# A macaron decoder layer: the feed-forward products by 2x2 blocks with seven block products, and the first input normed ahead of its products

## The chip, the core and the metric

One core of one Trainium2 chip runs the kernel. The metric is the device time of an execution in microseconds (us). Engines: PE (TensorE, matmuls; PEld its weight loads), DVE (VectorE), ACT (ScalarE), POOL (GpSimd), and SP, which issues most DMAs.

## The reference

One layer over 512 tokens of width 1024, all float32:

```python
def swiglu(x, w_gate, w_up, w_down):
    return (jax.nn.silu(x @ w_gate) * (x @ w_up)) @ w_down
...
        h = rmsnorm(x, ffn1_pre_g[l])
        x = x + FFN_RES * rmsnorm(swiglu(h, ffn1_w_gate[l], ffn1_w_up[l], ffn1_w_down[l]), ffn1_post_g[l])
        h = rmsnorm(x, mix_pre_g[l])
        p = h @ w_in[l]
...
        y = jnp.concatenate([y_rwkv, y_diff], axis=-1) @ w_o[l]
        x = x + rmsnorm(y, mix_post_g[l])
        h = rmsnorm(x, ffn2_pre_g[l])
        x = x + FFN_RES * rmsnorm(swiglu(h, ffn2_w_gate[l], ffn2_w_up[l], ffn2_w_down[l]), ffn2_post_g[l])
```

The feed-forward parts (FFN1 and FFN2) have a hidden width of 2816. Between them stands a mixer: one projection, RWKV-7 heads, differential attention heads, and one output projection.

## The kernel before

Every matmul operand is split into a high and a low part (float32r), `hi + lo`, by ACT (the copy `hi`) and DVE (the difference `lo`) in `split` and `split_to` (L192/L193 for weights, L198/L199 for activations). A product is then three matmuls, hi·hi, hi·lo, lo·hi (`mm3`, L204 to L206). The weights come from DRAM through two buffers `raw` of 128x1024 on SP's queue (`load_w`, L175), are split, and wait in three pairs `whi`, `wlo`.

Tokens and features are tiled by 128. In FFN1 and FFN2 the gate and the up product (`gu`) run over 22 feature tiles, two products each over 8 k tiles, with the weights as the stationary operand and 512 tokens as the moving one. `gate_up` (L319) forms silu(gate)·up from the two PSUM banks and splits it into `ah` and `al`. The down product (`block`) runs over the 22 feature tiles as k tiles, each for 4 token tiles and 2 column halves of 512, into eight PSUM banks `y`. The last k tiles are taken token tile by token tile (`tail`), so that the norms of one tile (`norms`, L246: square sums on ACT, z = y·gain and the residual sum `xo` on DVE, norm, transposes by PE into the next operand) run beside the products of the next.

FFN1 starts on x transposed in DRAM (`xt`): `ffn1_start` (L371) scales it by the gain, splits it and multiplies at once; the tokens' 1/rms is found beside it, with square sums on POOL (L403, L405), and multiplied in after the product (`rbc`). The mixer's first four projections and FFN2's first four tiles are done by token halves (`early`, L351, products of 256 columns), so that the first half needs the norms of two token tiles only. Some weights at these places are split on POOL (L190, L193).

`Streams` keeps several generators of steps, in order of priority, with planned times; it sets the order in which instructions are written. The framework takes this order as a priority and may let a later instruction go ahead whose operands it expects earlier; each engine then executes its own queue in order.

## Time and profile before

| | us |
|---|---|
| median of 3 runs | 1164.03 |
| lowest and highest | 1162.4, 1164.34 |
| span of the profiled execution | 1162.5 |
| FFN1, from the first product to the first of the projections | 5.2 to 387.8 |
| mixer and output projection | to 775.9 |
| FFN2, to its last product | to 1154.6 |

The page and the trace are of one profiled execution. Its span runs from its first to its last instruction. PE's busy time contains the overlap of pipelined matmuls, so that a pace is read from the starts or from counts in a stretch. A row of the timeline gives the start, the duration, engine, line, operation, what it writes and reads, and in brackets the engine's idle time before it.

### The profile page before, as it was taken

What the parts mean: (1) busy time and instruction counts of PE and PEld (TensorE: products, weight loads), DVE (VectorE), ACT (ScalarE), POOL (GpSimd) and SP (SyncE); (2) the same over time, 40 slices, a digit from 0 to 9 for tenths busy, and PEclk for the clock granted to TensorE, in tenths of its full rate; (3) what the DMA queues carried; (4) which work ended last, traced back from release to release, by engine and by line L of the source; (5) the groups of instructions that cost most, each with busy time, mean ns of one, the idle gap of its engine ahead of it and who ended that gap; (6) DMA issues with size and microseconds to landing.
All of it is one profiled execution on the core that took longest, in us unless ns stands there. A gap on an engine that the chain in (4) does not pass through costs nothing.

```text
span 1162.5 us, 13940 instructions
## 1 busy us (share of the span) xinstructions
PE 1119.6 (96%) x5600; PEld 889.2 (76%) x5600; DVE 553.4 (48%) x889; ACT 378.4 (33%) x630; POOL 149.3 (13%) x92
## 2 busy tenths in 40 slices
PE   7999999999999899999799999989999999999997
PEld 5888888888887876787576776669888888888885
DVE  7544444442224763787636758474333333332224
ACT  4423322232123474222332336343232222221123
POOL 5000000000004234344320200430000000000000
PEclk9999999999999999899889989998999999999999
DMA  7332222332223422223321203424222232223322
GB/s 261 109 99 96 91 91 98 100 93 91 91 99 119 150 74 73 59 48 117 90 57 46 62 22 127 140 101 138 93 91 91 95 104 91 91 91 96 104 91 91
DMA packets 49697, 112.46 MB, mean 97 GB/s; under 512 B 21336, under 2 KB 21720, under 8 KB 49632
## 3 DMA queue, kind: packets, MB, share of 16 engines
q1 hardware_dynamic: 46304, 104.15, 27.9%
q10 hardware_dynamic: 2608, 5.28, 1.3%
q0 software_dynamic: 720, 2.13, 0.6%
q8 instruction: 44, 0.72, 0.2%
q14 instruction: 21, 0.17, 0.0%
HBM read 102.14 MB, written 7.34 MB: 94 GB/s over the span
## 4 chain that ended last, share of the span: by engine, by line
PE 86%; DVE 8%; ACT 2%; DMA 2%; issue 1%; POOL 0%; SPq 0%; DVEq 0%; ACTq 0%; POOLq 0%
PE gu L205 13%; PE gu L206 13%; PE gu L204 13%; PE y L204 7%; PE y L205 7%; PE y L206 7%; PE pj L204 3%; PE pj L205 3%; PE pj L206 3%; PE sc L1151 2%; DVE tmp L935 1%; DVE xo L267 1%; PE Y L1037 1%; PE Y L1036 1%; PE s L889 1%; PE op L1179 1%
## 5 line engine op out<-in xcount | busy, mean ns | idle before, releaser
L192 ACT ACTIVATE whi<-raw 128x1024 fp32r<-128x1024 f32 x154 | 163.2, 1060 | 530.6 <-PE gu L205 222.4
L193 DVE TENSOR_TENSOR wlo<-raw,whi 128x1024 fp32r<-128x1024 f32 x130 | 163.9, 1262 | 249.2 <-ACT whi L192 247.0
L204 PE MATMUL gu<-h,whi 128*128 128x512 f32 x672 | 266.4, 397 | 5.2 <-ACT h L393 5.2
L205 PE MATMUL gu<-h,whi 128*128 128x512 f32 x672 | 267.1, 398 | 2.6 <-DVE h L396 2.6
L206 PE MATMUL gu<-h,wlo 128*128 128x512 f32 x672 | 266.3, 396 | 0.3 <-DVE wlo L193 0.3
L204 PEld LDWEIGHTS gu<-h,whi 128*128 128x128 f32 x672 | 127.3, 189 | 34.8 <-ACT h L393 5.2
L205 PEld LDWEIGHTS gu<-h,whi 128*128 128x128 f32 x672 | 127.2, 189 | 34.8 <-DVE h L396 5.5
L206 PEld LDWEIGHTS gu<-h,wlo 128*128 128x128 f32 x672 | 127.3, 189 | 30.1 <-DVE wlo L193 0.8
L204 PE MATMUL y<-whi,ah 128*128 128x512 f32 x336 | 132.7, 395 | 0.0
L206 PE MATMUL y<-whi,al 128*128 128x512 f32 x336 | 132.6, 395 | 0.0
L205 PE MATMUL y<-wlo,ah 128*128 128x512 f32 x336 | 132.5, 394 | 0.0
L193 POOL TENSOR_TENSOR wlo<-raw,whi 128x1024 fp32r<-128x1024 f32 (+1 forms) x29 | 70.7, 2442 | 107.7 <-ACT whi L192 107.5
L204 PE MATMUL pj<-hm,whi 128*128 128x512 f32 x184 | 80.7, 439 | 0.0
L205 PE MATMUL pj<-hm,whi 128*128 128x512 f32 x184 | 77.7, 422 | 0.0
L206 PE MATMUL pj<-hm,wlo 128*128 128x512 f32 x184 | 76.5, 416 | 0.0
L205 PEld LDWEIGHTS y<-wlo,ah 128*128 128x128 f32 x336 | 63.3, 188 | 14.8
L206 PEld LDWEIGHTS y<-whi,al 128*128 128x128 f32 x336 | 63.3, 188 | 14.8
L204 PEld LDWEIGHTS y<-whi,ah 128*128 128x128 f32 x336 | 63.3, 188 | 14.5
L190 POOL TENSOR_TENSOR whi<-raw,zero 128x1024 fp32r<-128x1024 f32 (+1 forms) x5 | 9.4, 1898 | 377.4 <-PE y L206 361.7
L325 DVE TENSOR_TENSOR sa<-gu,sa 128x512 f32<-128x512 f32 x22 | 15.2, 692 | 77.0 <-PE gu L206 70.3
L204 PEld LDWEIGHTS pj<-hm,whi 128*128 128x128 f32 x184 | 37.2, 202 | 12.7 <-issue 4.9
L329 DVE TENSOR_TENSOR sa<-gu,rbc 128x512 f32<-128x512 f32 x22 | 15.2, 690 | 66.0 <-PE gu L206 66.0
(325 smaller groups left out, 1404.8 us busy)
## 6 DMA issues: line engine op xcount, KB each, us to landing
raw<-in_wgu SPq DMA_DIRECT2D x82, 512.0 KB, 3.4
raw<-in_wd SPq DMA_DIRECT2D x44, 512.0 KB, 3.4
raw<-in_win SPq DMA_DIRECT2D x27, 512.0 KB, 3.5
xd<-xo SPq DMA_DIRECT2D x8, 512.0 KB, 2.8
raw<-in_wo SPq DMA_DIRECT2D x8, 512.0 KB, 3.5
xo<-xd SPq DMA_DIRECT2D x8, 512.0 KB, 4.3
xt<-in_xt SPq DMA_DIRECT2D x8, 256.0 KB, 5.4
xo<-in_x SPq DMA_DIRECT2D x4, 512.0 KB, 5.2
```

The source lines that it names most:

```text
L192: nc.scalar.activation(hi[:, :m], src, AF.Copy)
L193: (eng or nc.vector).tensor_tensor(out=lo[:, :m], in0=src, in1=hi[:, :m], op=ALU.subtract)
L204: mm(ps, lhsT=a[0], rhs=b[0], start=first, stop=False)
L205: mm(ps, lhsT=a[0], rhs=b[1], start=False, stop=False)
L206: mm(ps, lhsT=a[1], rhs=b[0], start=False, stop=last)
L267: nc.vector.scalar_tensor_tensor(out=xo[:, hs[i]], in0=z[:, hs[i]], scalar=r, in1=xo[:, hs[i]], op0=ALU.mult, op1=ALU.add)
L325: nc.vector.tensor_tensor(out=a, in0=ps[1], in1=s, op=ALU.mult)
L329: nc.vector.tensor_tensor(out=a, in0=ps[1], in1=rbc, op=ALU.mult)
L889: nc.tensor.matmul(pv[:, i, :, :], lhsT=BK[rs, c, :, :], rhs=self.XR[p][rs, c, e:e + 2, :], start=True, stop=True)
L935: nc.vector.tensor_tensor(out=tv, in0=a, in1=b, op=ALU.mult)
L1036: mm(yo, lhsT=XR[p][rs, c, 1, :], rhs=SV[rs, p, i, :], start=True, stop=False)
L1151: mm(sc[:, 0:n], lhsT=q[rs, t * P:(t + 1) * P], rhs=k_[rs, 0:n], start=True, stop=False)
```

## The change

Each FFN product is done as 2x2 blocks by the Strassen-Winograd scheme: seven block products instead of eight, with sums and differences of blocks ahead and behind. A new class `FFN` does this.

Gate and up: the moving operand is cut in two halves of k (4 k tiles each) and two halves of the tokens (256), the weights in the same halves of k and in pairs of feature tiles m and m + 11. The seven operands (`B11`, `T1`, `T2`, `B21`, `T3`, `B22`, `T4`) are formed once, by `feat`, from the transposed norm. The weight sums are formed by POOL for each pair and product (`g_weights`, p = 5, 6, 7, 3), then split by ACT and DVE (`parts`), three slots ahead (`AHEAD`). A slot is 4 k tiles x 3 matmuls of 256 columns, and there are 14 for a pair (7 products, gate and up). Products are accumulated in PSUM where the scheme adds them (p = 1, 6, 7, 4 share a bank), the rest is added by DVE in `g_out`.

Down: the activations are kept in float32 (`F`), cut in two halves of the tokens and two of k (11 tiles each), the weights in halves of columns. POOL forms the weight differences in place (`Tw`) and the activation sums in groups of four k tiles (`d_group`), ACT and DVE split them. A unit is one k tile of one product: 2 token tiles x 3 matmuls of 512 columns; the phases are (1,5) interleaved, 6, 2, (7,3) interleaved, 4. The first two token tiles are finished at the end of (7,3), the last two at the end of 4.

FFN1 no longer reads the transposed x: each token tile is loaded, normed, transposed and split like the other inputs (`start`), its products begin when the first two tiles are there, and `rbc`, `ffn1_start`, `token_scale` and `gate_up` are gone. FFN2's early tiles and their splitting on POOL are gone as well; the first projection's weights (`e0`) are requested after FFN1's last product. The output projection takes its last three k tiles by token tiles, not the last five. FFN's weights get six raw buffers (`RAWS`).

The diff, cut to its core:

```diff
...
-    a["xt"] = np.ascontiguousarray(g["x"].T).reshape(KT, P, T)
...
-        hi = pool.tile([P, n], F32R, tag=tag + "hi", name=tag + "hi")
-        lo = pool.tile([P, n], F32R, tag=tag + "lo", name=tag + "lo")
+        if tag == "w":
+            hi, lo = (pool.tile([P, n], F32R, tag="w", name=f"w{x}", bufs=6) for x in ("hi", "lo"))
+        else:
+            hi = pool.tile([P, n], F32R, tag=tag + "hi", name=tag + "hi")
+            lo = pool.tile([P, n], F32R, tag=tag + "lo", name=tag + "lo")
...
+        if feat is not None:
+            nc.vector.tensor_scalar(out=z, in0=xo, scalar1=r, scalar2=None, op0=ALU.mult)
+            yield 0.0, 0.8
+            yield from feat(t, z, tb)
+            S.mark(f"{key}z{t}")
+            S.mark(f"{key}h{t}", 1.2)
+            return
...
-            h1 = self.feature(hp, "h1")
-            with tc.tile_pool(name="a1", bufs=1, reuse_waits="tile") as ap, \
-                    tc.tile_pool(name="t1", bufs=1, reuse_waits="tile") as tp:
-                acts = [None] * NF
-                for f in range(NF):
-                    if f == 0:
-                        ps0, acc = self.ffn1_start(h1, bp, tp)
...
+                f1 = FFN(self, 1, fp, bp, hp, hx)
+                f1.inputs()
                 for t in range(NT):
-                    S.add(self.norms(S, br, t, "f", ys[t], True, A["x"], self.xd, hm, (0, 1)))
-                S.add(self.tail(S, "f", range(NT), kts[-nt:], acts, ws, ys, False, True))
-                for t in range(3):
-                    self.fetch(br, t, A["x"])
+                    S.add(f1.start(t, A["x"]))
+                S.add(f1.stream())
...
+                for t in range(NT):
+                    S.add(tail1(t))
+                S.run("f")
+                xst.close()
                 e0 = self.load_w(A["win"][0], nc.gpsimd, alone=True)
...
+            f2 = FFN(self, 2, fp, fp, hp, hx)
+            f2.inputs()
+            br = self.bridge(f2.bridge_tile(), fp, "pgm")
...
-            nt = 5
+            nt = 3
...
+            S.add(f2.stream())
...
+    NP = NF // 2
+    AHEAD = 3
+    LAG = 4
+    HS = "xppxpxp"
...
+    def parts(self, src, dst, lo=None):
+        nc = self.nc
+        nc.scalar.activation(dst[0], src, AF.Copy)
+        (lo or nc.vector).tensor_tensor(out=dst[1], in0=src, in1=dst[0], op=ALU.subtract)
...
+        x = self.x0[:, t * D:(t + 1) * D]
+        junk = self.x0[:, 4 * D:5 * D]
+        nc.sync.dma_start(out=x, in_=src[t * P:(t + 1) * P, :])
+        if t < 2:
+            self.load(0, t, 0)
+        else:
+            for j in range(2):
+                self.load(0, j, 1) if t == 3 else None
+        yield 0.0, 2.0
+        r = L.rms(x, junk, "p")
+        yield 0.0, 2.5
+        nc.vector.tensor_scalar(out=x, in0=x, scalar1=r, scalar2=None, op0=ALU.mult)
+        yield 0.0, 0.6
+        yield from self.feat(t, x, (4, 5) if t < 2 else (0, 1))
+        S.mark(f"oh{t}", 1.2)
...
+            hv = self.h32[:, q * 2 + half, :, cs]
+            g = L.fv[:, o + q * 4:o + q * 4 + 4].unsqueeze(2).to_broadcast([P, 4, P])
+            nc.vector.tensor_tensor(out=hv, in0=pt.rearrange("p (k t) -> p k t", k=4), in1=g, op=ALU.mult)
+            if half == 0:
+                self.parts(hv, dst(("B11", "B21")[q]))
+            yield 0.42, 0.3 if q == 0 else 0.0
+        if half == 0:
+            return
+        B11, B12, B21, B22 = (self.h32[:, i, :, cs] for i in range(4))
+        t1, t2, t3, t4 = (self.gsum(p).rearrange("p (k t) -> p k t", k=4) for p in (3, 3, 7, 7))
+        tt = lambda e, o, a, b: e.tensor_tensor(out=o, in0=a, in1=b, op=ALU.subtract)
+        tt(nc.vector, t1, B12, B11)
+        self.parts(t1, dst("T1"))
+        tt(nc.gpsimd, t2, B22, t1)
+        self.parts(t2, dst("T2"))
+        self.parts(B22, dst("B22"))
+        tt(nc.gpsimd, t3, B22, B12)
+        self.parts(t3, dst("T3"))
+        tt(nc.gpsimd, t4, B21, t2)
...
+    RAWS = 6
+    ALPHA, BETA, GAMMA = ((4, 5), (2, 3)), (6, 7), (0, 1)
+    OPERAND = {1: "B11", 2: "B21", 3: "B22", 4: "T4", 5: "T1", 6: "T2", 7: "T3"}
...
+        if p == 1:
+            return raw(0)[:, lo]
+        if p == 2:
+            return raw(0)[:, hi]
+        if p == 4:
+            return raw(1)[:, hi]
+        s = self.gsum(p)
+        tt = lambda a, b, op: nc.gpsimd.tensor_tensor(out=s, in0=a, in1=b, op=op)
+        if p == 5:
+            tt(raw(1)[:, lo], raw(1)[:, hi], ALU.add)
+        elif p == 6:
+            tt(self.s[j][5], raw(0)[:, lo], ALU.subtract)
+        elif p == 7:
+            tt(raw(0)[:, lo], raw(1)[:, lo], ALU.subtract)
+        else:
+            tt(raw(0)[:, hi], self.s[j][6], ALU.subtract)
+        self.s[j][p] = s
+        return s
...
+        out = [(0, 1), (0, 2), (1, 1), (1, 2), (0, 5), (0, 6), (0, 3), (0, 7), (1, 5), (0, 4), (1, 6), (1, 3), (1, 7),
+               (2, 1), (1, 4)]
+        for m in range(2, self.NP):
+            out += [(m, p) for p in (5, 6, 2, 7, 3)]
+            out += [(m + 1, 1)] if m + 1 < self.NP else []
+            out.append((m, 4))
+        return [(m, p, j) for m, p in out for j in range(2)]
...
+        for k in range(4):
+            ks = slice(k * P, (k + 1) * P)
+            mm(ps, lhsT=w[:, 0, ks], rhs=B[:, 0, k], start=p in (1, 2, 5) and k == 0, stop=False, skip_group_check=True)
+            mm(ps, lhsT=w[:, 0, ks], rhs=B[:, 1, k], start=False, stop=False, skip_group_check=True)
+            mm(ps, lhsT=w[:, 1, ks], rhs=B[:, 0, k], start=False, stop=k == 3, skip_group_check=True)
...
+        if p == 6:
+            nc.scalar.activation(c0[:, 1], ps, AF.Copy)
+        elif p == 2:
+            add(c0[:, 0])
+        elif p == 7:
+            add(c1[:, 1])
+            if j == 0:
+                nc.scalar.activation(c1[:, 1], c1[:, 1], AF.Silu)
+        elif p == 3:
+            add(c0[:, 1])
+            if j == 0:
+                nc.scalar.activation(c0, c0, AF.Silu)
+            else:
+                nc.vector.tensor_tensor(out=self.F[0][:, :, m], in0=c0, in1=self.c[m, 0, 0], op=ALU.mult)
+        elif j == 0:
+            nc.scalar.activation(c1[:, 0], ps, AF.Silu)
+        else:
+            g1 = self.c[m, 0, 1]
+            nc.gpsimd.tensor_tensor(out=self.F[1][:, 1, m], in0=c1[:, 1], in1=g1[:, 1], op=ALU.mult)
+            nc.vector.tensor_tensor(out=self.F[1][:, 0, m], in0=ps, in1=g1[:, 0], op=ALU.mult)
...
+        for ph in ((1, 5), (6,), (2,), (7, 3), (4,)):
+            if len(ph) == 1:
+                out += [(ph[0], k) for k in range(n)]
+                continue
+            for k in range(n + g):
+                out += [(ph[0], k)] if k < n else []
+                out += [(ph[1], k - g)] if k >= g else []
...
+        if p == 1:
+            raw = self.fp.tile([P, 1024], F32, tag="raw", name="raw", bufs=self.RAWS)
+            nc.sync.dma_start(out=raw, in_=self.wd[k])
+            self.raw[k] = raw
+            return raw[:, lo]
+        if p == 5 or p == 4:
+            return self.Tw[:, k]
+        if p in (6, 2):
+            if k % 2 == 0:
+                self.raw[p, k // 2] = self.d_raw(k, *((n + i, int(p == 6)) for i in range(k, min(k + 2, n))))
+            src = self.raw[p, k // 2][:, (lo, hi)[k % 2]]
+            if p == 6:
+                sub(self.Tw[:, k], src, self.Tw[:, k])
+                return self.Tw[:, k]
+            return src
+        if p == 7:
+            self.raw["c", k] = raw = self.d_raw(k, (k, 1), (n + k, 1))
+            sub(raw[:, lo], raw[:, hi], raw[:, lo])
+            return raw[:, lo]
+        return self.raw["c", k][:, hi]
...
+        if p == 5:
+            tt(a21, a21, a22, ALU.add)
+        elif p == 6:
+            tt(a21, a21, a11)
+        elif p == 7:
+            tt(a11, a22, a21)
+        elif p == 3:
+            tt(a21, a12, a21)
+        src = {1: a11, 2: a12, 4: a22, 5: a21, 6: a21, 7: a11, 3: a21}[p]
+        t = self.hslot("a")
+        self.parts(src, (t[:, 0, 0:n], t[:, 1, 0:n]))
...
+        for t in tts:
+            ts = slice(t * P, (t + 1) * P)
+            a = [A[:, i, k % 4, ts] for i in range(2)]
+            mm(ps[t], lhsT=a[0], rhs=w[:, 0], start=p in (1, 2, 5) and k == 0, stop=False, skip_group_check=True)
+            mm(ps[t], lhsT=a[0], rhs=w[:, 1], start=False, stop=False, skip_group_check=True)
+            mm(ps[t], lhsT=a[1], rhs=w[:, 0], start=False, stop=k == n - 1, skip_group_check=True)
...
+            ahead(i + self.AHEAD)
+            self.g_product(m, p, j, ws.pop(i))
+            self.g_out(m, p, j)
+            yield 1.43, 0.0
...
+                if p == 1:
+                    nc.gpsimd.tensor_tensor(out=self.Tw[:, k], in0=self.raw[k][:, 512:1024],
+                                            in1=self.raw[k][:, 0:512], op=ALU.subtract)
+                if p == 2:
+                    nc.gpsimd.tensor_tensor(out=self.Tw[:, k], in0=self.raw[2, k // 2][:, (k % 2) * 512:(k % 2) * 512 + 512],
+                                            in1=self.Tw[:, k], op=ALU.subtract)
...
+        for i, (p, k) in enumerate(units[:-nt]):
+            prep(i + self.AHEAD)
+            self.d_product(p, k, ws.pop(i))
+            if k == self.NP - 1:
+                self.d_out(p)
+            if (p, k) == (3, self.NP - 1):
+                a, c1, c5, c6 = self.d_bank(4), self.c[1], self.c[5], self.c[6]
+                self.y = [[c1[:, t], c6[:, t]] for t in range(2)] + [[a[t], c5[:, t]] for t in range(2)]
+                S.mark(key + "e")
...
+        for t in range(2):
+            for i in range(nt):
+                p, k = units[i0 + i]
+                self.d_product(p, k, ws[i0 + i], (t,))
+                yield 0.7, 0.0
+            S.mark(f"{out}y{t + 2}", 0.2)
...
```

## Rows read from the trace of the kernel before

**Rows 1.** the page, busy time of the engines, and two of its 40-slice rows

```profile
PE 1119.6 (96%) x5600; PEld 889.2 (76%) x5600; DVE 553.4 (48%) x889; ACT 378.4 (33%) x630; POOL 149.3 (13%) x92
POOL 5000000000004234344320200430000000000000
PEclk9999999999999999899889989998999999999999
```

**Rows 2.** the page, the chain that ended last, shares of the span by engine

```profile
PE 86%; DVE 8%; ACT 2%; DMA 2%; issue 1%; POOL 0%; SPq 0%; DVEq 0%; ACTq 0%; POOLq 0%
```

**Rows 3.** FFN1's stretches: busy us (count) of PE, PEld, DVE, ACT, POOL; clock; DMA

```profile
100.00:200.00 100.00, 100.00 (x432) 81.07 (x431) 45.15 (x54) 29.30 (x36) 0.00 (x0) 1.00 0.29 95
275.00:360.00 85.00, 85.00 (x368) 68.92 (x367) 20.74 (x17) 17.92 (x17) 0.00 (x0) 1.00 0.32 106
```

**Rows 4.** the timeline, PE (start, us): first down product of FFN1, last of FFN2

```profile
260.44 0.39 PE L204 MATMUL y<-whi,ah 128*128 128x512 f32 x1
1154.41 0.40 PE L206 MATMUL y<-whi,al 128*128 128x512 f32 x1
```

**Rows 5.** the timeline, PE: first products, 256 columns, of FFN2's first two tiles

```profile
775.90 0.28 PE L359 MATMUL gu<-h,eghi 128*128 128x256 f32 x1
778.77 0.28 PE L359 MATMUL gu<-h,euhi 128*128 128x256 f32 x1
```

**Rows 6.** groups by line and shape: count, busy us, mean ns, idle before

```profile
L199 DVE TENSOR_TENSOR al<-sa,ah 128x512 fp32r<-128x512 f32 x44 | 30.1, 685 | 1.4 <-ACT ah L198 1.4
L193 DVE TENSOR_TENSOR wlo<-raw,whi 128x1024 fp32r<-128x1024 f32 x130 | 163.9, 1262 | 249.2 <-ACT whi L192 247.0
L896 DVE TENSOR_TENSOR AM<-s,mask 128x256 f32<-128x256 f32 x16 | 6.7, 416 | 0.2
L198 ACT ACTIVATE ah<-sa 128x512 fp32r<-128x512 f32 x44 | 27.7, 632 | 17.3 <-DVE sa L330 13.7 <-DVE sa L325 3.6
```

**Rows 7.** the timeline, POOL and DVE: alone, and beside one another

```profile
363.03 2.40 POOL L193 TENSOR_TENSOR wlo<-raw,whi 128x1024 fp32r<-128x1024 f32 x1
365.39 1.89 POOL L190 TENSOR_TENSOR ew1hi<-raw,zero 128x1024 fp32r<-128x1024 f32 x1
366.55 1.39 DVE L260 TENSOR_TENSOR z<-y,row_pg 128x512 f32<-128x512 f32 x2 [8.26 <-ACT junk L258]
416.60 2.36 POOL L193 TENSOR_TENSOR wlo<-raw,whi 128x1024 fp32r<-128x1024 f32 x1 [6.99 <-ACT whi L192]
417.07 2.43 DVE L193 TENSOR_TENSOR sh2lo<-sh,sh2hi 128x512 fp32r<-128x512 f32 x1 [2.17 <-ACT sh2hi L192]
740.19 1.57 DVE L193 TENSOR_TENSOR ewlo<-raw,ewhi 128x1024 fp32r<-128x1024 f32 x1 [0.19 <-ACT ewhi L192]
740.76 3.27 POOL L193 TENSOR_TENSOR eglo<-raw,eghi 128x1024 fp32r<-128x1024 f32 x1
741.68 3.43 DVE L193 TENSOR_TENSOR salo<-raw,sahi 128x1024 fp32r<-128x1024 f32 x1
```

**Rows 8.** the timeline, DVE and POOL, at the start of the kernel

```profile
15.70 6.59 DVE L396 SCALAR_TENSOR_TENSOR h<-xt,fv,h 128x512 fp32r<-128x512 f32 x4
18.30 5.13 POOL L405 TENSOR_TENSOR sq<-sq 128x512 f32<-128x512 f32 x3
```

**Rows 9.** busy time by stretches, the first 25 us

```profile
0.00:25.00 25.00, 16.85 (x52) 11.29 (x53) 20.33 (x24) 13.11 (x20) 17.16 (x15) 1.00 0.76 255
```

**Rows 10.** the timeline, PE: first product of all, first of the mixer's projections

```profile
5.18 0.80 PE L204 MATMUL gu<-h,whi 128*128 128x512 f32 x1 [5.18 <-ACT h L393]
387.79 0.28 PE L359 MATMUL pe<-hm,whi 128*128 128x256 f32 x1
```

**Rows 11.** the timeline, PE: transposes ahead of FFN2, with the idle time before

```profile
786.48 0.87 PE L294 MATMUL pt<-ident,xn 128*128 128x128 f32 x3 [5.99 <-DVE xn L284]
```

**Rows 12.** the timeline, PE: two neighbouring products near the start

```profile
8.34 0.63 PE L206 MATMUL gu<-h,wlo 128*128 128x512 f32 x1
8.77 0.63 PE L204 MATMUL gu<-h,whi 128*128 128x512 f32 x1
```

More of the change, by code (lines that the diff above doesn't have):

```diff
@@ L265, in norms @@
         yield 0.0, 1.6
+        last = h is None and feat is None
         for i in range(2):
@@ L485, in run @@
                     self.block(ys[t], YK[k], w, t, i == 0, False)
[L486 to L487 removed]
+            ws = [self.load_w(A["wo"][k]) for k in kts[-nt:]]
             for t in range(NT):
[L489 removed]
+                S.add(self.norms(S, br, t, "o", ys[t], False, self.xd, self.xd, None, (0, 1), f2.feat))
             S.add(self.tail(S, "o", range(NT), kts[-nt:], YK, ws, ys, False, True))
@@ L512, in run @@
-            S.add(early())
-            S.run()
-            est.close()
-            ap = self.ap
-            bp = st.enter_context(tc.tile_pool(name="br3", bufs=1, reuse_waits="tile"))
-            br = self.bridge(bp, "pg2")
-            for f in range(2, NF):
-                ps = self.gu(A["wgu2"], f, h2)
-                acts[f] = self.gate_up(f, ps, ap, tp, None)
-            kts = list(range(4, NF)) + list(range(4))
-            nt = 3
-            ys = [[self.bank(b, "y") for _ in range(2)] for b in ((0, 1), (4, 5), (6, 7), (2, 3))]
```

384 lines of the change are left out of this document (220 added, 164 removed).

## The prediction

> **What bounds the kernel now.** I read the page first: TensorE is busy for 96% of the span, POOL for 13%, and POOL's slices are empty wherever the two feed-forward parts (FFN1, FFN2) run [rows 1]. The chain that ended last is 86% PE [rows 2]. The table by stretches then shows that inside the gate/up and the down stretches PE never waits: 432 matmuls of 512 columns in 100.00 us and 368 in 85.00 us, which is 0.2315 us for one, with VectorE (DVE) at 45% and 24%, ScalarE (ACT) at 29% and 21%, and POOL at nothing [rows 3]. So these parts are bound by the number of matmul columns, and a transform that removes one product in eight attacks the right thing, as long as what it adds elsewhere stays under PE.
>
> **What FFN costs now.** Gate and up: 2 x 22 tiles x 8 k tiles x 3 = 1056 matmuls x 0.2315 = 244.5 us. Down: 22 x 4 x 2 x 3 = 528 x 0.2315 = 122.2 us. Sum 366.7 us, twice. In FFN1 the first down product starts at 260.44 [rows 4], so gate/up behaves as if it had begun, dense, at 260.44 - 244.5 = 15.9; this is the price of the start. In FFN2 the last product ends at about 1154.6 [rows 4], so its dense start is 1154.6 - 366.7 = 787.9.
>
> **Step 1, PE alone.** After: gate/up is 11 x 7 x 2 = 154 slots of 12 matmuls with 256 columns; down is 77 units of 6 with 512 columns. A 256-column matmul does not cost half: 24 of them stand between two tiles' first ones at 775.90 and 778.77, 0.1196 us each [rows 5]. So gate/up is 1848 x 0.1196 = 221.0 and down is 462 x 0.2315 = 107.0. By PE alone the change saves 23.5 + 15.2 = 38.7 us per FFN, 77.4 us in all: 14% of the columns, but 10.5% of the time.
>
> **Step 2, what it adds on DVE and POOL.** Weights and operands are now split in halves that are first added or subtracted. Per pair m of feature tiles (14 slots, 14 x 1.435 = 20.1 us of PE): 14 low parts on DVE (128x512, two SBUF operands) and one product of that size; six additions that read PSUM and one small product; 8 sums of 128x512 on POOL and one product of 256. Rows: the low part takes 0.685 us alone, an operation of 256 columns from PSUM 0.416, and ACT's copy 0.632 [rows 6]. ACT needs some 12 of the 20.1 us and is no bound.
>
> DVE and POOL, however, do not add up as two engines. Where both work on SBUF operands, one waits for the other's whole instruction: a low part of 128x512 that starts at 417.07 ends 0.54 us after POOL's instruction (418.96 to 419.50), taking 2.43 instead of 0.69; at the out-projection DVE's 1024-column low part takes 3.43, ending 1.08 after POOL's, and POOL's takes 3.27, ending 2.27 after DVE's [rows 7]. In contrast two DVE operations with one operand in PSUM take 1.39 together, their usual time, under a POOL instruction [rows 7]. At the start of the kernel, where both have work in stock, they alternate: three POOL instructions in 5.13 us (1.71 each), four of DVE in 6.59 (1.65 each) [rows 8]. I call this the lock, and what an instruction holds it for its turn: 0.54 us for DVE's 512 columns, 1.71 - 0.54 = 1.17 for POOL's; 1.08 and 2.27 for 1024.
>
> The Trainium skill ("SBUF — State Buffer", section "Who interferes with whom") has a rule for this: the two share one port pair under an exclusive lock, a DVE instruction with two SBUF inputs contends with a POOL instruction that reads SBUF, and one with at most one SBUF input does not. By that rule the sums below hold only for the low parts, the POOL sums and the few products from SBUF, and not for the additions out of PSUM; the rows agree (1.39 for the two). The same skill ("Perfetto Trace Analysis", "Optimizing Scalar/DVE Operations") warns that moving work from one of the two to the other might not help, which speaks against this change.
>
> **Gate/up with the lock.** Per m: 15 x 0.54 + 8 x 1.17 + 0.6 (estimate from half of the 512 one) = 18.1 us of turns under 20.1 us of PE, 90%. It fits, with little room: the low parts run three slots (4.3 us) ahead of PE. Ends: no stall, 221.0; and DVE sitting out every POOL instruction and paying 0.69 for each of its own, 15 x 0.69 + 7 x 0.42 + 8 x 1.17 + 0.6 = 23.3 per m, 256. I take 225, near the lower end, since PE's need exceeds the turns' and POOL's sums depend on weights alone, so that it can keep ahead. Change: -19.5 (ends -23.5 and +11.5).
>
> **Down with the lock.** The units run in the phases (1,5), 6, 2, (7,3), 4. DVE: one low part per unit, and three groups (1024, 1024, 768 columns) for each of seven operands. POOL: 44 sums of 128x512 (one per unit of 1, 6, 2 and 7) and three group sums for each of 5, 6, 7 and 3. Up to the end of (7,3): DVE 66 x 0.54 + 6 x (1.08 + 1.08 + 0.82) = 53.5; POOL 44 x 1.17 + 4 x (2.27 + 2.27 + 1.71) = 76.5; together 130.0 us of turns, while PE needs 66 x 1.389 = 91.7. This stretch is bound by the lock. Phase 4 has no POOL work: 11 x 1.389 = 15.3. With 2 us to fill at the beginning: 147.3, against 122.2 now: +25.1. Ends: PE alone, 107.0 (-15.2), and 167 if each instruction costs its full duration (0.69, 1.26 and 2.40 [rows 6, 7], and an estimated 1.3 for POOL's 512) with no overlap at all (+45). I take the sum of turns, as it is what the alternating rows show [rows 8].
>
> So an FFN costs 225 + 147.3 = 372.3, 5.6 more than now; both, +11.2.
>
> **The start.** x is loaded token-major, squared, scaled, transposed, and only then multiplied. 512 KB take 2.1 us at the 255 GB/s of the first stretch [rows 9], so data are not late for long. DVE's list before slot 8, the first that needs all tokens: 4 scalings (0.8 each, an estimate from the 0.69 rows), 8 evacuations, 4 + 12 parts and differences, 10 weight parts: 3.2 + 34 x 0.69 = 26.7 us, from about 6.5 on, and half of POOL's six 1.17 on top: 37; the first of the operands is ready some 3 before: 34. Slots 0 to 7 (11.5 us) are done under it, so the dense start is 22.5 instead of 15.9: +6. Ends 0 (loads bound it as now) and +20 (the engines take the four token tiles in the order of the code, all transposes ahead of the first product). First product: at about 14 instead of 5.18 [rows 10].
>
> **FFN1 to the mixer.** Dense, FFN1's products would end at 382.6; the first product of the projections starts at 387.79 [rows 10]: 5.2 lost to norms and transposes. After, token tiles 0 and 1 are finished a phase earlier (15.3 us of cover), but tiles 2 and 3 come 2.8 us apart and the first projection weights are requested later. The four early projections (24 x 0.1196 = 2.9 us each) cover the second half. I take 0, ends -3 and +6. The mixer is unchanged.
>
> **Mixer to FFN2.** Now the dense start (787.9) is 12.0 after the first FFN2 product at 775.90 [rows 5]; the worst gap in it is 5.99 us of PE waiting for a norm [rows 11]. After: DVE has per token tile 7.2 us (tiles 0, 1) and 10.0 us (tiles 2, 3, with differences and parts), 34.4, and 11 weight parts, 7.6, and about 3 behind POOL: 45, beginning 12.5 us before the out-projection's end (three token tiles of 4.2): 32 after it, 29 for the first operand; minus 11.5 for slots 0 to 7: 17. Against 12: +5. Ends 0 (the out-projection loses some 3 us of waits, as POOL no longer splits weights beside it) and +14.
>
> The end of the kernel is the same chain behind the last token tile: 0.
>
> **Sum.** 2 x (-19.5 + 25.1) + 6 + 0 + 5 = +22.2. On the profiled span, 1162.5 + 22.2 = 1184.7. The median of the runs, 1164.03, is 1.5 above that span, so 1186.
>
> **Rivals.**
> (a) Faster, PE alone decides: the lock bites less than counted, because DVE and POOL get enough ahead of PE. Then 1164 - 77.4 + 11 = 1098. For it: gate/up's turns fit under PE. Against: in down the turns exceed PE's time by 38 us, and nothing can be prepared far ahead with six raw buffers. 10%.
> (b) Faster, part of it: gate/up without stalls (-23.5) and the 11 subtractions of phase 1, which need weights alone, done in gate/up's spare turns (11 x 1.17 = 12.9 off, down +12): 2 x (-11.5) + 11 = -12, 1152. It decides if that memory is free before gate/up ends; it shares its place with gate/up's buffers. 13%.
> (c) No change within 0.2%: 5%.
> (d) Slower still: gate/up is bound by DVE's queue behind POOL's sums, 23.3 us per m: 256 instead of 225, 2 x 31 on top, 1248. It decides once POOL's sums come in bursts longer than the three slots of lead. 8%.
> (e) PE, waiting in each down unit, is granted the lower of its two levels (1.2 instead of 2.4 GHz): among the first matmuls, at that pace, one takes 0.43 us [rows 12]; a unit is then 2.56 us, more than the 1.9 of the lock; 77 x 2.56 = 197, 2 x 50 on top, 1286. The clock of the tight stretches stays at nine tenths or more now [rows 1], so 4%.
> That the change doesn't run seven products is excluded by its lists (154 slots, 77 units).
>
> **How the numbers follow.** My forecast, 1166 to 1212, has 60%. 0.2% is about what a measurement of this kernel can tell from no change. Faster: (a) and (b), 0.23; same 0.05; slower 0.72. The range from 1135 to 1228 holds the forecast, (b) and (c), and leaves out (a), (e) and most of (d).
>
> **What would show it.** Right: in down PE is busy for about three quarters, its gaps end with DVE's low parts, and DVE's 128x512 low parts take about 1.7 us there instead of 0.69, while in phase 4 they fall back to 0.69 and PE is dense. Gate/up: about 20.5 us for 14 slots. Wrong: a down stretch near 107 us, or low parts at 0.69 beside a busy POOL; then the lock was over-counted and (a) or (b) holds. A first dense slot far from 22 us would show the start mis-sized.

## The result, and the profile after

The changed kernel takes 1224.7 us (median of 4 runs, 1224.0 to 1232.0) against 1164.2 of the kernel before on the same chip: a ratio of 1.051, interval 1.045 to 1.057, or 60.5 us more. The forecast was 1186. The profiled execution of the changed kernel spans 1222.7 us, 60.2 more than that of before. The page, busy time of the engines and three of its rows in 40 slices, beside [rows 1]:

```profile
PE 1088.4 (89%) x6972; PEld 925.2 (76%) x6972; DVE 1007.2 (82%) x1353; ACT 588.7 (48%) x1151; POOL 662.4 (54%) x391
...
DVE  6989999999996955677943777379789999999967
...
POOL 3867786869972433524231210015867787699730
PEclk9799999998899898978989999987999999989999
```

PE has less to do, as planned, but is idle for 11% of the span. In the feed-forward parts, where POOL had nothing to do and DVE was busy for 24 to 45% before [rows 3], DVE is now nearly full and POOL busy for about three quarters of the time. The timeline, PE, beside [rows 4, 5, 10]: FFN1's first product behind 28 slots (two pairs' worth), its first and last down product, the projections' first product of the unbroken run, the last of the output projection, then the same three places of FFN2.

```profile
81.67 0.29 PE L602 MATMUL gu<-T,w 128*128 128x256 f32 x1
...
265.49 0.39 PE L721 MATMUL y<-w,a 128*128 128x512 f32 x1
...
413.26 0.39 PE L723 MATMUL y<-w,a 128*128 128x512 f32 x1
...
427.95 0.56 PE L351 MATMUL pe<-hm,whi 128*128 128x256 f32 x1
...
812.59 0.40 PE L210 MATMUL y<-whi,yt 128*128 128x512 f32 x1
...
883.62 0.28 PE L602 MATMUL gu<-T,w 128*128 128x256 f32 x1
...
1066.29 0.39 PE L721 MATMUL y<-w,a 128*128 128x512 f32 x1
...
1215.87 0.40 PE L723 MATMUL y<-w,a 128*128 128x512 f32 x1
```

From these marks the forecast can be settled term by term. The dense start is the first of these marks minus two pairs, 28 slots, at the steady pace (20.16 us in FFN1, 20.06 in FFN2, from the starts of products 14 slots apart).

| term, us | forecast | measured | difference |
|---|---|---|---|
| FFN1, dense start | 22.5 | 81.67 - 40.3 = 41.4 | +18.9 |
| FFN1, gate/up | 225 | 265.49 - 41.4 = 224.1 | -0.9 |
| FFN1, down | 147.3 | 148.0 | +0.7 |
| FFN1's last product to the projections | 5.2 | 14.5 | +9.3 |
| mixer to the output projection's end | 388.1 | 385.0 | -3.1 |
| FFN2, dense start after it | 17 | 883.62 - 40.1 - 813.0 = 30.5 | +13.5 |
| FFN2, gate/up | 225 | 222.8 | -2.2 |
| FFN2, down | 147.3 | 149.8 | +2.5 |
| end of the kernel | 7.9 | 6.6 | -1.3 |

The differences sum to 37.4; 1184.7 + 37.4 = 1222.1, the span but for 0.6, which is the forecast's own rounding (22.5 - 15.9 = 6.6 went into its sum as 6). So the two large steps, gate/up and down, came out as forecast, and the miss stands in three places: the two starts (32.4) and the way from FFN1 to the mixer (9.3).

The table by stretches (busy us and count of PE, PEld, DVE, ACT, POOL; clock; DMA) of the changed kernel: the start, a steady stretch of gate/up, and down by its five phases, cut at the starts of its 1st, 133rd, 199th, 265th and 397th matmul.

```profile
26.00:46.00 20.00, 6.20 (x39) 5.40 (x38) 19.44 (x17) 7.37 (x14) 16.45 (x10) 0.65 0.10 27
...
86.00:106.00 20.00, 20.00 (x169) 20.00 (x168) 17.65 (x23) 11.49 (x23) 14.89 (x9) 1.00 0.31 106
...
265.49:321.18 55.69, 40.06 (x134) 28.02 (x133) 55.69 (x32) 23.16 (x36) 54.62 (x28) 0.88 0.40 128
321.18:347.63 26.45, 19.19 (x68) 13.47 (x66) 26.45 (x17) 10.74 (x17) 24.95 (x14) 0.91 0.16 50
347.63:363.99 16.36, 16.36 (x67) 13.15 (x66) 16.30 (x17) 9.75 (x15) 10.52 (x5) 0.94 0.61 191
363.99:398.03 34.04, 32.77 (x133) 24.46 (x132) 23.50 (x33) 15.99 (x28) 8.56 (x6) 1.00 0.38 125
398.03:413.49 15.46, 15.46 (x67) 12.24 (x65) 14.71 (x20) 9.14 (x20) 6.71 (x3) 1.00 0.14 46
```

Gate/up is as dense as in [rows 3]. Down up to the end of (7,3) takes 132.5 us, against 130.0 of turns and 2 to fill in the forecast. The sum came out, its places did not: by the forecast's turns the four phases would take 37.0, 28.0, 21.8 and 43.2 us, and they took 55.7, 26.4, 16.4 and 34.0. POOL ran ahead and did most of its sums in (1,5) and 6, where DVE and POOL are both full and PE waits; counted with the instructions that really fell there, the turns of these two phases are about 56 and 27 us (an estimate from the forecast's prices). In 2 and (7,3) POOL has 11 sums left and PE is nearly dense; in phase 4, without sums, it is dense. The groups by line and shape (count, busy us, mean ns, idle before) say why; first from 266 to 392, then from 392 to 413:

```profile
L722 PE MATMUL y<-w,a 128*128 128x512 f32 x124 | 55.6, 448 | 23.6 <-DVE w L479 23.4
...
L479 DVE TENSOR_TENSOR w<-raw,w 128x512 fp32r<-128x512 f32 x41 | 44.1, 1114 | 9.3 <-ACT w L478 9.2
L479 DVE TENSOR_TENSOR w<-Tw,w 128x512 fp32r<-128x512 f32 x22 | 39.8, 1842 | 0.0
...
L777 POOL TENSOR_TENSOR Tw<-raw 128x512 f32<-128x512 f32 x11 | 19.8, 1821 | 0.0
...
L479 DVE TENSOR_TENSOR w<-Tw,w 128x512 fp32r<-128x512 f32 x11 | 7.3, 685 | 1.1 <-ACT w L478 1.1
```

The low part of the same tile `Tw` takes 1.84 us beside POOL's sums and 0.685 without them, and PE's gaps end with it. The low parts out of `raw`, most of which fall where POOL has less to do, take 1.11; all 63 together 1.37 at the mean. In gate/up (82 to 242 us) they are held up too, only that PE doesn't wait for it:

```profile
L479 DVE TENSOR_TENSOR w<-s,w 128x512 fp32r<-128x512 f32 x65 | 71.9, 1139 | 7.3 <-ACT w L478 7.3
...
L564 POOL TENSOR_TENSOR s<-raw 128x512 f32<-128x512 f32 x33 | 55.4, 1697 | 41.7 <-DMA raw<-in_wgu 37.3 <-DVE w L479 4.4
...
L619 DVE TENSOR_TENSOR c<-gu,c 128x256 f32<-128x256 f32 x49 | 20.2, 412 | 0.1
```

The last row is the addition with one operand in PSUM: 0.412 us, as long as alone [rows 6], beside a POOL that is busy for three quarters of the time. That agrees with the rule of the Trainium skill ("SBUF — State Buffer", "Who interferes with whom") that a DVE instruction with at most one SBUF input, outside its 2-port modes, does not contend with POOL. The prediction left that exception out, and one kind of instruction here is held up although it reads only one tile from SBUF: the scaling of a token tile, 0.75 us alone, took 1.76 beside POOL's sums at FFN1's start. Whether it runs in such a mode no run here shows.

```profile
18.47 1.76 DVE L498 TENSOR_SCALAR F<-F,pr 128x1024 f32<-128x1024 f32 x1
```

### The profile page after: what moved, and what is told of

Its sections match the earlier page's. It is cut to its first block, busy times and chain, and to the rows that moved or that the text cites. A ratio compares the mean times of both kernels' runs of the same rounds, so it can differ in the third digit from the quotient of the medians.

```text
span 1222.7 us, 18685 instructions
## 1 busy us (share of the span) xinstructions
PE 1088.4 (89%) x6972; PEld 925.2 (76%) x6972; DVE 1007.2 (82%) x1353; ACT 588.7 (48%) x1151; POOL 662.4 (54%) x391
## 3 DMA queue, kind: packets, MB, share of 16 engines
q1 hardware_dynamic: 55376, 117.72, 30.2%
## 5 line engine op out<-in xcount | busy, mean ns | idle before, releaser
L479 DVE TENSOR_TENSOR w<-raw,w 128x512 fp32r<-128x512 f32 x220 | 250.1, 1155 | 25.0 <-ACT w L478 23.4
L564 POOL TENSOR_TENSOR s<-raw 128x512 f32<-128x512 f32 x88 | 144.1, 1656 | 180.1 <-DMA raw<-in_wgu 104.8
L602 PE MATMUL gu<-T,w 128*128 128x256 f32 x704 | 201.1, 286 | 19.4 <-ACT T L478 10.8
L479 DVE TENSOR_TENSOR w<-s,w 128x512 fp32r<-128x512 f32 x176 | 194.2, 1138 | 21.0 <-ACT w L478 20.8
L603 PE MATMUL gu<-T,w 128*128 128x256 f32 x704 | 200.3, 285 | 3.7 <-DVE T L479 3.7
L604 PE MATMUL gu<-T,w 128*128 128x256 f32 x704 | 200.3, 285 | 0.0
L478 ACT ACTIVATE w<-raw 128x512 fp32r<-128x512 f32 x220 | 135.1, 627 | 113.5 <-PE gu L604 45.4
L722 PE MATMUL y<-w,a 128*128 128x512 f32 x308 | 132.6, 431 | 49.8 <-DVE w L479 49.0
L604 PE MATMUL gu<-B,w 128*128 128x256 f32 x528 | 151.8, 288 | 5.1 <-DVE w L479 5.1
L602 PE MATMUL gu<-B,w 128*128 128x256 f32 x528 | 151.5, 288 | 1.4 <-ACT B L478 1.4
L603 PE MATMUL gu<-B,w 128*128 128x256 f32 x528 | 151.2, 287 | 1.2 <-DVE B L479 1.2
L602 PEld LDWEIGHTS gu<-T,w 128*128 128x128 f32 x704 | 134.3, 191 | 20.8 <-ACT T L478 11.7
L603 PEld LDWEIGHTS gu<-T,w 128*128 128x128 f32 x704 | 134.9, 192 | 4.3 <-DVE T L479 4.3
L604 PEld LDWEIGHTS gu<-T,w 128*128 128x128 f32 x704 | 134.1, 190 | 0.0
L721 PE MATMUL y<-w,a 128*128 128x512 f32 x308 | 127.1, 413 | 4.7 <-ACT w L478 4.5
L478 ACT ACTIVATE w<-s 128x512 fp32r<-128x512 f32 x176 | 110.0, 626 | 41.8 <-POOL s L564 18.3
L723 PE MATMUL y<-w,a 128*128 128x512 f32 x308 | 126.2, 410 | 0.0
L604 PEld LDWEIGHTS gu<-B,w 128*128 128x128 f32 x528 | 101.9, 194 | 5.6 <-DVE w L479 5.6
L603 PEld LDWEIGHTS gu<-B,w 128*128 128x128 f32 x528 | 102.8, 195 | 1.9 <-DVE B L479 1.9
L602 PEld LDWEIGHTS gu<-B,w 128*128 128x128 f32 x528 | 102.3, 194 | 1.6 <-ACT B L478 1.6
```

Source lines behind the costliest of these rows:

```text
L478: nc.scalar.activation(dst[0], src, AF.Copy)
L479: (lo or nc.vector).tensor_tensor(out=dst[1], in0=src, in1=dst[0], op=ALU.subtract)
L564: tt = lambda a, b, op: nc.gpsimd.tensor_tensor(out=s, in0=a, in1=b, op=op)
L602: mm(ps, lhsT=w[:, 0, ks], rhs=B[:, 0, k], start=p in (1, 2, 5) and k == 0, stop=False, skip_group_check=True)
L603: mm(ps, lhsT=w[:, 0, ks], rhs=B[:, 1, k], start=False, stop=False, skip_group_check=True)
L604: mm(ps, lhsT=w[:, 1, ks], rhs=B[:, 0, k], start=False, stop=k == 3, skip_group_check=True)
```

## The experiments

All are made from the changed kernel. The forecast's theory is the lock: DVE's instructions with two SBUF operands and POOL's exclude each other. One place of caution: the mixer, which no edit touches but for its first weights' splits, took between 382 and 396 us in these profiles, so that differences of a few us are read from the stretch that was edited, not from the total. The starts scatter too: the five kernels with the starts unedited, the changed one among them, have dense starts of 41.4 to 44.0 us in FFN1 and 30.5 to 31.4 in FFN2.

### Is the down stretch bound by the lock?

Three kernels. The first moves down's sums from POOL to DVE:

```diff
-        sub = lambda o, a, b: nc.gpsimd.tensor_tensor(out=o, in0=a, in1=b, op=ALU.subtract)
+        sub = lambda o, a, b: nc.vector.tensor_tensor(out=o, in0=a, in1=b, op=ALU.subtract)
...
-        tt = lambda o, a, b, op=ALU.subtract: nc.gpsimd.tensor_tensor(out=o, in0=a, in1=b, op=op)
+        tt = lambda o, a, b, op=ALU.subtract: nc.vector.tensor_tensor(out=o, in0=a, in1=b, op=op)
...
-                    nc.gpsimd.tensor_tensor(out=self.Tw[:, k], in0=self.raw[k][:, 512:1024],
+                    nc.vector.tensor_tensor(out=self.Tw[:, k], in0=self.raw[k][:, 512:1024],
...
-                    nc.gpsimd.tensor_tensor(out=self.Tw[:, k], in0=self.raw[2, k // 2][:, (k % 2) * 512:(k % 2) * 512 + 512],
+                    nc.vector.tensor_tensor(out=self.Tw[:, k], in0=self.raw[2, k // 2][:, (k % 2) * 512:(k % 2) * 512 + 512],
```

> The changed kernel with every sum of the down products (44 of weights, 12 of activations, for each feed-forward part) on DVE instead of POOL. Theory of the lock: DVE now has 110 instructions of 512 columns at 0.685 us and 30 of 768 or 1024 at 1.05 to 1.35 up to the end of (7,3), 113 us, then 15.3 for phase 4 and 2 to begin: a down stretch of 130 us instead of 148 to 150, low parts at 0.69, and 1187 us for the kernel instead of 1225. Rival 1, DVE's low parts are slow on their own: the work moved adds 45 us to an engine that was busy all the time, down 193, kernel 1313. Rival 2, down waits for its loads: no change, 1225.

Measured: 1155.7 us, ratio to before 0.988 (0.979 to 0.996); down 112.7 and 113.9 us. The table by stretches, from 264 to 360 (down's phases up to (7,3) end at 361.3):

```profile
264.00:360.00 96.00, 93.37 (x393) 72.59 (x392) 95.75 (x142) 57.72 (x91) 0.00 (x0) 1.00 0.48 165
```

The groups by line and shape in it:

```profile
L479 DVE TENSOR_TENSOR w<-raw,w 128x512 fp32r<-128x512 f32 x41 | 27.1, 681 | 0.0
L479 DVE TENSOR_TENSOR w<-Tw,w 128x512 fp32r<-128x512 f32 x26 | 17.3, 678 | 0.0
```

Giving the fullest engine 56 more instructions per feed-forward part shortened the stretch by 35 us. Both rivals fall. The expected 130 was itself too long: behind one another, DVE's instructions of 512 columns start 0.60 us apart, not 0.685 (1.28 us for two in its timeline), so that DVE is busy for 97 us up to the end of (7,3), close to PE's 91.7.

The second leaves the sums out, the third lets POOL do as many on a tile of its own:

```diff
-                sub(self.Tw[:, k], src, self.Tw[:, k])
-                return self.Tw[:, k]
+                return src
...
-            sub(raw[:, lo], raw[:, hi], raw[:, lo])
...
-                    nc.gpsimd.tensor_tensor(out=self.Tw[:, k], in0=self.raw[k][:, 512:1024],
-                                            in1=self.raw[k][:, 0:512], op=ALU.subtract)
...
+                    nc.sync.dma_start(out=self.Tw[:, k], in_=self.wd[k][:, 512:1024])
```

```diff
+            self.nc.gpsimd.tensor_tensor(out=self.scr, in0=self.scr, in1=self.scr, op=ALU.subtract)
```

> Leaves out all sums of weights and activations in the down products (the operands are the plain blocks, the second half of the weights is loaded once more), so that POOL has nothing to do there; all products, low and high parts stay. Theory of the lock: DVE's 77 low parts at 0.685 and 21 groups at 1.05 to 1.4 are 79 us under PE's 107: PE is dense, down about 110 us, kernel 1147. Rival, down is bound by loads, by the six buffers for them or by the way from ACT to DVE to PE: down stays above 135, kernel above 1195.

> Leaves out all sums in the down products as the run e3_down_nosums did, but lets POOL do as many sums of 512 columns (44 and 24) on a tile of its own that nobody reads or waits for. It tells the lock from a chain in which PE only waits for POOL's results. Theory of the lock: each of POOL's instructions still keeps DVE's low parts out, these take 1.7 us while POOL runs, and the down stretch is 135 to 145 us instead of 108, kernel some 1195 to 1210. Rival, POOL's results were what DVE waited for: low parts at 0.69, down 108, kernel 1138.

Measured: without sums 1138.1 us, down 108.2 and 107.8, as expected and as PE alone needs (107.0). With the idle sums 1205.1 us, down 139.6 and 140.2. The table by stretches, first of the kernel without sums, then of the one with idle sums while POOL works:

```profile
264.00:360.00 96.00, 96.00 (x413) 77.26 (x412) 67.98 (x96) 60.91 (x98) 0.00 (x0) 1.00 0.53 185
```

```profile
266.00:365.00 99.00, 77.82 (x301) 55.21 (x299) 99.00 (x68) 46.76 (x74) 93.98 (x65) 0.97 0.48 158
```

The groups of the one with idle sums, in that stretch, and in the last line after POOL has ended (366 to 404):

```profile
L709 POOL TENSOR_TENSOR scr<-scr 128x512 f32<-128x512 f32 x65 | 94.5, 1454 | 5.1
L479 DVE TENSOR_TENSOR w<-raw,w 128x512 fp32r<-128x512 f32 x37 | 54.8, 1521 | 0.0
...
L479 DVE TENSOR_TENSOR w<-Tw,w 128x512 fp32r<-128x512 f32 x11 | 7.4, 687 | 2.0 <-ACT w L478 2.0
```

Nobody waits for the scratch sums, yet PE stands still again and the low parts take 1.5 us. So in down it is not POOL's results that come late, nor loads or buffers: POOL's mere activity on SBUF holds DVE up. That is 32 of the 40 us between 108 and 148; the other 8 are not told apart (here POOL runs ahead of the products and takes 512 columns at a time).

### From FFN1 to the mixer

```diff
-                e0 = self.load_w(A["win"][0], nc.gpsimd, alone=True)
+                e0 = self.load_w(A["win"][0])
...
-                w.append(L.load_w(src[j], nc.gpsimd, *((lp, f"ew{j}") if j in (1, 2) else ()), alone=j < 5))
+                w.append(L.load_w(src[j], nc.gpsimd if j >= EARLY else None, *((lp, f"ew{j}") if j in (1, 2) else ()), alone=j == 4))
```

> The changed kernel with the weights of the first four projections split by ACT and DVE instead of POOL. Theory of the lock at this place: seven DVE instructions of the norms, 15.9 us in all beside POOL's splits, take 0.73 each, against three or four low parts of 1.26 more: the first product of the projections comes 7 us sooner after FFN1's last one (14.3 us now), kernel 1218. Rival, the norms of the last token tiles wait for each other or for these weights, not for POOL: no change or later, 1225 or more.

Measured: 1213.3 us, ratio 1.038 (1.029 to 1.047), 11.4 less than the changed kernel; the gap is 3.6 us instead of 14.5. Groups of the norms in the changed kernel (406 to 424):

```profile
L288 DVE SCALAR_TENSOR_TENSOR F<-z,or,F 128x512 f32<-128x512 f32 x2 | 5.2, 2633 | 0.0
L306 DVE SCALAR_TENSOR_TENSOR F<-F,pr,row_gm 128x512 f32<-128x512 f32 x2 | 4.9, 2458 | 0.0
...
L197 POOL TENSOR_TENSOR ew1lo<-raw,ew1hi 128x1024 fp32r<-128x1024 f32 x1 | 2.9, 2851 | 0.0
```

and in this one (408 to 424):

```profile
L288 DVE SCALAR_TENSOR_TENSOR F<-z,or,F 128x512 f32<-128x512 f32 x4 | 2.9, 746 | 0.0
...
L306 DVE SCALAR_TENSOR_TENSOR F<-F,pr,row_gm 128x512 f32<-128x512 f32 x2 | 1.5, 750 | 0.0
```

The splits that before ran on POOL beneath FFN1's products (363.03 and 365.39 in [rows 7]) stand behind FFN1's last product in the changed code; in its trace they run from 406.7 to 422.6, on the norms that the projections wait for. Theory held; the gain was larger than the expected 7.

### The two starts

First everything of POOL's in the feed-forward parts goes to DVE, also the operands' differences in `feat`, the weight sums of `g_weights` and the small product in `g_out`:

```diff
-        tt(nc.gpsimd, t2, B22, t1)
+        tt(nc.vector, t2, B22, t1)
...
-        tt = lambda a, b, op: nc.gpsimd.tensor_tensor(out=s, in0=a, in1=b, op=op)
+        tt = lambda a, b, op: nc.vector.tensor_tensor(out=s, in0=a, in1=b, op=op)
...
-            nc.gpsimd.tensor_tensor(out=self.F[1][:, 1, m], in0=c1[:, 1], in1=g1[:, 1], op=ALU.mult)
+            nc.vector.tensor_tensor(out=self.F[1][:, 1, m], in0=c1[:, 1], in1=g1[:, 1], op=ALU.mult)
```

> The changed kernel with no POOL work in the feed-forward parts at all: sums of weights, operands and activations all on DVE. Theory of the lock, at the two starts too: down 130 as in the run before; gate/up has 22 x 0.685 + 6 x 0.41 + 1.5 = 19.1 us of DVE for 20.1 of PE and stays dense; the starts lose their slow low parts, so the first product with T1 comes some 12 us earlier in FFN1 (52.9 now) and 10 earlier in FFN2: 1165 us. Rival 1, the starts are late because DVE's list is long: six more differences and the sums make them 4 to 8 us later, kernel some 1195. Rival 2, gate/up becomes DVE-bound without POOL's help: 24 us per pair instead of 20.1, two times 40 more, 1245.

Measured: 1133.6 us, ratio 0.968 (0.961 to 0.976). The starts fell from 41.4 to 32.8 and from 30.5 to 21.5, by 8.6 and 9.0 us; gate/up kept 20.2 us per pair, DVE alone carrying all of it. Then two kernels try the order, `ahead` five slots in advance instead of three, one with POOL's work, one without:

```diff
-        for i in range(self.AHEAD):
+        for i in range(5):
             ahead(i)
...
-            ahead(i + self.AHEAD)
+            ahead(i + 5)
```

> The changed kernel, POOL's work kept, with gate/up's weights split five slots ahead of the products instead of three. Theory of the order: at the start of FFN1 the low parts of the first weights stand in DVE's queue behind the operands T1 and T2, so that PE has nothing to do from 29 to 44 us; two more slots split before that let the first eight slots pass under it, and the dense start moves from 41.4 to about 32, in FFN2 some 4 us of a later stall go: 1212 us. Theory of the lock alone: T1 itself is late, the order doesn't matter, 1225.

> No POOL work in the feed-forward parts, and weights five slots ahead. Where PE waited 8.5 us for the low part of a weight (FFN1, with everything on DVE) and 3.8 in FFN2, it should wait no more: dense start of FFN1 from 32.4 to 24, of FFN2 3 earlier, 1122 us instead of 1133.5. Rival, DVE is the bound of the start (28 us without a pause from 17 on) and any order only moves the wait to T1: no change, 1133.

Measured: with POOL 1222.3 us and starts of 42.2 and 30.2, no gain (1224.7, 41.4, 30.5). Without POOL 1132.1 us and starts of 29.9 and 22.3, against 32.8 and 21.5: 3 us of the expected 8 in FFN1, none in FFN2, and the kernel's time stays. As the bound of the starts, the order falls in both kernels. Loading all of x first, and on top of it the scaling on ACT, were tried on the best kernel (below):

```diff
...
+        if t == 0:
+            for u in range(4):
+                nc.sync.dma_start(out=self.x0[:, u * D:(u + 1) * D], in_=src[u * P:(u + 1) * P, :])
+            for half in range(2):
+                for j in range(2):
+                    self.load(0, j, half)
```

```diff
-        nc.vector.tensor_scalar(out=x, in0=x, scalar1=r, scalar2=None, op0=ALU.mult)
+        nc.scalar.activation(x, x, AF.Copy, scale=r)
...
-            nc.vector.tensor_scalar(out=z, in0=xo, scalar1=r, scalar2=None, op0=ALU.mult)
+            nc.scalar.activation(z, xo, AF.Copy, scale=r)
```

> As f3_best, but the four token tiles of x are loaded ahead of the first weights in FFN1. There DVE has some 5 us of work in the first 15 us, as it waits for tokens that are loaded between weights (squares of the second tile at 8.9, of the last at 14.3), and works without a pause from then on. Theory: the start is a late begin plus DVE's list, so tokens that are complete 3 us earlier move the dense start from 30 to 27 us: kernel 1115 against 1118. Rival: the first weights, now later, hold the first eight slots and thereby the start: no gain or up to 3 us more.

> As g1_x_first, and the scaling of the tokens by 1/rms, four instructions of 0.75 us on DVE at each of the two starts, is done by ACT instead. Theory, DVE's list is the bound of both starts: 3 us less in each, 1109 against 1115. Rival, ACT has squares, high parts and evacuations in the same stretch and its queue takes DVE's place: no change.

Measured: 1119.1 and 1117.9 us beside 1118.0, dense starts of FFN1 31.1 and 31.1 beside 30.0, of FFN2 22.6 and 19.1 beside 21.3. Both expectations fell: with x first the first product comes sooner (15.8 instead of 20.0), but PE then waits 6.5 us for a low part behind the operands in DVE's queue; with the scaling on ACT only FFN2's start gained, 2.2 of the expected 3. Another kernel returns gate/up's sums of weights and its small product to POOL and is else the best one:

> As f3_best, but gate/up's sums of weights (8 for each pair) and its small product are POOL's again, while the differences of the operands and all of the down products' sums stay on DVE. It tells what the lock costs in a stretch where the turns of both (18.1 us per pair) fit under PE (20.1), and which of POOL's work at the starts was in the way. Theory: gate/up's steady stretch stays dense at 20.1 us per pair; at each start only the first pair's sums meet DVE's list, some 5 instructions of 1.2 us, so the starts come 3 to 5 us later than in f3_best: 1125 against 1118. Rival 1, DVE is relieved of 8 sums per pair and the starts gain: 1113. Rival 2, POOL's sums stall the steady stretch: over 1140.

Measured: 1136.8 us, ratio 0.976 (0.971 to 0.980), 19 more than the best kernel. The first product behind 28 slots, in FFN1 and FFN2, in the best kernel, then in this one:

```profile
70.35 0.28 PE L602 MATMUL gu<-T,w 128*128 128x256 f32 x1
...
811.94 0.28 PE L602 MATMUL gu<-T,w 128*128 128x256 f32 x1
```

```profile
77.88 0.29 PE L602 MATMUL gu<-T,w 128*128 128x256 f32 x1
...
837.85 0.35 PE L602 MATMUL gu<-T,w 128*128 128x256 f32 x1
```

With the output projections ending at 750.5 and 767.4, the starts are 30.0 and 21.3 in the best kernel, 37.6 and 30.3 here: 7.6 and 9.0 us, 16.6 of the 19 and more than the expected 3 to 5 each, are the price of the weight sums (and the small product) on POOL at the starts. For FFN2 that is all that the start had gained by the move to DVE; the operands' differences cost little there. The price is not the lock alone. PE's longest single wait in FFN2's start of the changed kernel, 4.59 us, ends a chain from POOL's sum over ACT's high part and DVE's low part, while DVE itself stands idle for 4.41:

```profile
862.69 0.63 ACT L478 ACTIVATE w<-s 128x512 fp32r<-128x512 f32 x1 [4.60 <-POOL s L564]
863.36 1.07 DVE L479 TENSOR_TENSOR w<-s,w 128x512 fp32r<-128x512 f32 x1 [4.41 <-ACT w L478]
864.82 0.43 PE L602 MATMUL gu<-T,w 128*128 128x256 f32 x1 [4.59 <-DVE c L619]
```

Here POOL's results do come late. The kernels that move the sums take away both, the lock and the lateness, and do not tell them apart. The steady stretch is unhurt, but it shows who pays; the best kernel, then this one:

```profile
72.00:232.00 160.00, 160.00 (x1336) 160.00 (x1335) 140.35 (x256) 93.08 (x184) 0.00 (x0) 1.00 0.32 106
```

```profile
80.00:238.00 158.00, 158.00 (x1318) 157.97 (x1317) 147.88 (x176) 90.82 (x182) 115.47 (x74) 1.00 0.34 105
```

PE is dense in both. DVE is busy for 88% of the time when it does all the sums itself, and for 94% when POOL does them for it.

### The version that beats both

All on DVE, five slots ahead, early splits on ACT and DVE.

> No POOL work in the feed-forward parts, weights five slots ahead, and the first four projections' weights split by ACT and DVE: the three places are separate stretches, so that the gains should add: 1133.5 - 11 (order) - 11 (projections, as with POOL's sums kept) = 1111 us. Rival, with POOL idle beside the down products the early splits no longer disturb the norms, and their gain is already spent: 1122.

Measured: 1118.0 us (1114.3 to 1123.0), ratio to before 0.959 (0.955 to 0.963). The expected 1111 was missed by what the order was to give. The gains add as far as they exist: 1133.6 - 11.4 = 1122, and nothing from the order; the 4 below that are within the mixer's scatter. The rival's number, 1122, fits as well, but not its reason: the gap to the mixer fell from 15.2, with everything of the feed-forward parts on DVE, to 3.9, so the early splits' gain was not spent. FFN1 and FFN2 have down stretches of 112.8 and 113.0 and starts of 30.0 and 21.3.

## Why the prediction was right or wrong

**Direction right, mechanism right in the two large steps, size wrong.** Of the 60.2 us, gate/up and down together are 11.3 (forecast 11.2), the two starts 44.0 (forecast 11), the way from FFN1 to the mixer 9.3 (forecast 0) and the rest -4.4. In down the lock gives back what seven products save, as forecast: 147.3 against 148.0 and 149.8, with the signs named ahead: low parts of 1.8 us on `Tw`, PE's gaps ending with them, 0.69 and a dense PE in phase 4. The sum of turns from the alternating rows [rows 8] held, though POOL's sums crowded into the first two phases; that POOL's activity holds DVE up there is shown by the idle sums.

**Gate/up: right.** 224.1 and 222.8 against 225, dense at the pace of the 256-column matmuls [rows 5]. Rival (d), a DVE queue of 23.3 us per pair, did not come: DVE was busy for 17.7 of 20 us.

**The starts: the terms that were mis-sized.** FFN1 +6 became 25.5 (41.4 - 15.9), FFN2 +5 became 18.5 (30.5 - 12). The first step that failed is the sum of DVE's list at 0.69 an instruction, with POOL put in at "half of POOL's six 1.17" and, in FFN2, at "about 3". I had priced the low parts by turns in gate/up and down, but by their time alone here, where DVE has the longest list of all. Moved to DVE, POOL's work there was worth 8.6 and 9.0 us at the starts, and the weight sums with the small product alone 7.6 and 9.0. That those sums depend on weights only, which I had counted in their favour in gate/up, is no help at the starts.

The second failing step is an overlap: "Slots 0 to 7 (11.5 us) are done under it", and a dense PE from T1 on. FFN1's start in the changed kernel, the low part of T1, the wait behind it, and the next product with T1:

```profile
39.43 0.58 PE L603 MATMUL gu<-T,w 128*128 128x256 f32 x1 [2.70 <-DVE T L479]
44.44 0.58 PE L604 MATMUL gu<-B,w 128*128 128x256 f32 x1 [4.43 <-DVE w L479]
...
53.11 0.28 PE L604 MATMUL gu<-T,w 128*128 128x256 f32 x1
```

T1's low part was used at 39.43 (forecast 34). Then PE waited until 44.44 for the low part of a weight of the first eight slots, which stood behind the operands in DVE's queue, and 54 of these slots' 96 matmuls were still to do; they ended at 53.11, and from there PE is dense. With no POOL at all T1 is used at 31.61, sooner than forecast, but 34 of the 96 are left, and the start is still 30.0 and not 22.5: the first product comes at 20.0 instead of 14, and PE waits 4.9 us for parts of T1 and of a weight. That kernel already splits five slots ahead (32.8 with three); x first gained nothing more. In FFN2 the first eight slots were done in time and T1 came 31.2 us after the output projection (forecast 29); there 10.8 us are lost behind T1, 4.59 of them on the late sums shown above and some on the clock.

The clock: while PE waits, the granted clock falls (0.65 in the row from 26 to 46), and the first products after the wait run at the lower level, 0.21 us apart instead of 0.12:

```profile
44.82 0.41 PE L602 MATMUL gu<-B,w 128*128 128x256 f32 x1
45.03 0.41 PE L603 MATMUL gu<-B,w 128*128 128x256 f32 x1
```

The changed kernel's timeline has 35 such pairs in FFN1's start and 65 in FFN2's, some 3.3 and 6.1 us at 0.094 each. Rival (e) had the clock, and its 0.43 us for 512 columns is what a granted clock of 0.50 shows from 281.4 to 288.1; but it was granted for part of down only (0.88 in (1,5), 1.00 in (7,3)), and the stretch stayed at its turns.

**FFN1 to the mixer: wrong.** I took 0 with ends -3 and +6; it was +9.3. "The first projection weights are requested later" stood in the text, but I looked at the loads, not at where their splits on POOL would fall: on seven norm instructions, 15.9 us instead of 5. The run with these splits on ACT and DVE shows it.

**Mixer to FFN2, its first part.** The output projection became 4 us shorter, the lower end that I had named: its products run from 711.2 to 775.9 before and from 752.1 to 813.0 after. POOL's splits beside it [rows 7] are gone and its last k tiles are taken in another order; no run tells the two apart.

**The rivals.** (a) PE alone would give 1098; moving POOL's work off comes to 1118. There gate/up and down take 334.6 and 333.7 us instead of 366.7: 65 of the 77 us counted by PE alone, the rest being down at DVE's list. The starts take 23 of it back. Of (b) one half came, a gate/up without stalls; the other, phase 1's subtractions in gate/up's spare turns, did not: they stand in the rows of down. Two readings of the prediction are wrong without moving its sum: one product in eight is 12.5% of the columns, not 14%, and of the two DVE operations "under a POOL instruction" only the first was, as that instruction ended at 367.28 [rows 7]; the 49 additions in gate/up carry that reading.

## What to carry to other kernels

A helper that shares a path with the engine it relieves must be priced by what it takes from that engine: here DVE's low parts and products grew by 55 us beside 74 POOL instructions in the steady gate/up stretch of the kernel with POOL's weight sums (0.74 each, from the groups by shape against those of the best kernel), and by 58 us beside 52 in down of the changed kernel (1.1 each, against the kernel with down's sums on DVE), while DVE does a sum of 512 columns in 0.60; the work given to the idle engine made the busy one busier. Use one price for an interaction in every stage where both engines work, above all at starts and boundaries, where the list of the bound engine is longest and nothing runs ahead. And when a request is moved, follow every instruction that it triggers to the place where it will now run.
